# A hybrid decoder layer on one core: the instruction order taken from a simulation in time of queues and engines

## The chip, the cores and the metric

The kernel runs on one core of a Trainium2 chip. The metric is the device time of one execution in microseconds (us), the median of several runs. The engines are PE (TensorE, matmuls; PEld is its weight load), DVE (VectorE), ACT (ScalarE), POOL (GpSimd) and SP (SyncE, which here issues nearly all transfers). Each engine has its own list of instructions, and waits on semaphores for the others.

## The reference

One layer of a decoder with two groups of heads side by side, over 2048 tokens of width 1024, in float32:

```
h = rmsnorm(x);  z = h @ W_in                    # q, k, v and gates of both groups
FoX,   8 heads x 64:  softmax(q k^T * scale + c_t - c_s, causal) @ v
                      # c: running sum of log forget gates; swept in blocks of 128 queries
mLSTM, 4 heads x 128: 16 chunks of 128 tokens, each
       num = w_inter * (q @ C) + ((q k^T) * w_intra) @ v
       C   = decay * C + (wk * k)^T @ v          # carried from chunk to chunk
       h   = num / max(|den|, exp(-m))           # times sigmoid(output gate), after a norm
x += concat(groups) @ W_out
x += relu(rmsnorm(x) @ W_up)^2 @ W_down
x += sigmoid(rmsnorm(x) @ W_pg) * (p @ W_ple);   out = rmsnorm(x)
```

q and k of the mLSTM pass through a causal convolution of width 4 and a SiLU first.

## The kernel before

All of the layer is one function, hybrid_layer, written with a tile framework: the code names tiles from pools and issues operations in program order, and the framework's scheduler decides in which order each engine gets its instructions, and puts in the semaphore waits. A pool gives a tag a number of buffers (bufs); a new tile of that tag waits until the readers of the tile that had the buffer are done. Products with full precision are made from several f16 products (high and low parts, names with hl), three matmuls where there was one.

The stages, in the order of the program:

- Start: x is normalized in groups of four token blocks (squares yjk on ACT, yy on ACT and DVE, L181 to L201) and transposed on SP (yt); the weights of mLSTM head 0 are scaled (L140, L155), and the gates of all heads computed.
- mLSTM, heads 0 to 3. ml_z makes the projections of a head: zqk (matmuls at L260, 128x512, into u), zvo (L271, 128x256, into va by L454 on ACT and og by L455 on DVE), and the convolution of q and k on DVE (L469, L471, two tiles of 128x2048). All use the PSUM pool psz with 4 banks. qk has 4 buffers, so two heads; va and og have one for even and one for odd heads. Then the head's 16 chunks run (below).
- After the chunks of a head: a normalization on DVE (mrd, mss, mrr; L534 to L541), sixteen products (L544), mh on ACT and POOL (L546, L547), and on SP two transposes mT (L550) and two stores mixd (L552).
- FoX: fox_z makes v, k and q for two heads at a time (zv at L271, zfk and zfq at L260). fox_attn then takes each head's query blocks in pairs of 17 key blocks: s on PE (L798, L800), bias added and maximum on DVE (L806), exp on ACT (L821), f16 parts on ACT and POOL (ph, L826, L828), transposes pt on SP (L830, 17 for each head), and av on PE (L846). av trails s by LAG = 3 pairs. The projections of later heads, the per-layer embedding products (pp) and part of the output projection (om) are written between the pairs as fill.
- Output projection (L641), MLP (h at L1036, d at L1054), the gate (pg at L1007) and the final norm.

A chunk c of mLSTM head h, shortened:

```
A.activation(wt[:, c, :], wt[:, c, :], AF.Exp, ...)                        # L498
PE.matmul(sps, lhsT=k[:, cc], rhs=q[:, cc], ...)                           # L500 s
V.scalar_tensor_tensor(wt[:, c, :], sps, scale, wt[:, c, :], MULT, MULT)   # L501
PE.matmul(nps, lhsT=wt[:, c, :], rhs=va[:, c, :], ...)                     # L504 n
PE.matmul(ips, lhsT=q[:, cc], rhs=cst, ...)                                # L508 i
PE.transpose(out=kps, in_=k[:, cc], ...)                                   # L519 k
A.activation(kw, kps, AF.Copy, scale=w_k[:, c, h:h + 1])                   # L521
PE.matmul(cps, lhsT=kw, rhs=va[:, c, :], ...)                              # L523 c
V.scalar_tensor_tensor(cn, cst, dec[...], cps, MULT, ADD)                  # L526 cst
```

wt of a head is loaded by SP from mrow (L490) and has mneg added on DVE (L492) before the exp. wt and mh share one buffer: both are allocated with tag="w", bufs=1. What of the later projections stands on PE between these matmuls is the scheduler's choice; in the order before it spreads them over the chunks.

The scheduler is chosen where the tile framework is opened, in the function below.

## Time and profile before

| | us |
|---|---|
| time, median of 3 runs | 2955.1 (2953.64 to 2956.42) |
| the profiled execution: its own time | 2954.4 |
| its span | 2952.7 |
| PE busy | 2698.4 |
| DVE busy | 1621.7 |
| ACT busy | 1008.3 |
| POOL busy | 698.7 |

The profile is of one execution. Busy times are sums over the instructions of an engine; the span less the busy time of PE is the time in which PE waited or had nothing to do.

### The profile page before, as it was taken

Reading aid. Unit: us, or ns where it says so; the run is one execution under the profiler, and the core shown is the slowest. Engines: PE = TensorE matmul, PEld = TensorE weight load, DVE = VectorE, ACT = ScalarE, POOL = GpSimd, SP = SyncE. Lnnn points to the kernel's source line nnn. Section 1 sums busy time; section 2 is a strip of 40 time slices with the busy share of each in tenths; the row PEclk is TensorE's granted clock in tenths of the full one; section 3 lists DMA queues with packets and bytes.
Section 4 is the critical chain, followed back from the end, with each engine's and each line's share of the span. In section 5 each row is a group of like instructions: output and inputs, shape, how many; then the busy total and the mean of one; then the engine's idle time right before and its main releaser. Section 6 shows DMA issues by size and latency. Waiting matters only on the chain. (4 is left out here: it accounts for less than half of the span.)

```text
span 2952.7 us, 45034 instructions
## 1 busy us (share of the span) xinstructions
PE 2698.4 (91%) x18229; PEld 1507.1 (51%) x18229; DVE 1621.7 (55%) x3633; ACT 1008.3 (34%) x1686; POOL 698.7 (24%) x435
## 2 busy tenths in 40 slices
PE   4998999888878788788999999999999999999997
PEld 2756767555454554343344444444444444444686
DVE  6464654766757657556654444444444444445636
ACT  6244444465555555553411111111111111113532
POOL 1011110244343444343122111111212111111132
PEclk9999999989899989999999999999999999999999
DMA  9212220387686879996700000000000000002623
GB/s 243 45 44 59 58 47 20 94 167 137 139 166 133 165 169 219 196 205 222 148 29 29 29 29 16 28 15 29 29 29 29 29 29 16 28 15 43 143 69 136
DMA packets 535265, 256.36 MB, mean 87 GB/s; under 512 B 432784, under 2 KB 502672, under 8 KB 535056
## 3 DMA queue, kind: packets, MB, share of 16 engines
q1 hardware_dynamic: 525296, 236.66, 35.0%
q10 hardware_dynamic: 9760, 16.82, 1.8%
q8 instruction: 142, 2.33, 0.3%
q14 instruction: 67, 0.55, 0.1%
HBM read 113.88 MB, written 32.60 MB: 50 GB/s over the span
## 5 line engine op out<-in xcount | busy, mean ns | idle before, releaser
L1054 PE MATMUL d<-wd_hl,hid 128*128 128x512 f16 x3072 | 678.2, 380 | 8.4 <-DVE x L1059 8.2
L1036 PE MATMUL h<-y1t,wu_hl 128*128 128x512 f16 x3072 | 673.5, 379 | 0.5 <-issue 0.5
L1054 PEld LDWEIGHTS <-hid 128*128 128x128 f16 x3072 | 301.3, 98 | 375.0 <-issue 15.8
L1036 PEld LDWEIGHTS <-wu_hl 128*128 128x128 f16 x3072 | 300.5, 98 | 363.2 <-ACT y1y L200 1.0
L1059 DVE SCALAR_TENSOR_TENSOR x<-d,fac,x 128x512 f32<-128x512 f32 x512 | 373.8, 747 | 132.2 <-PE d L1054 131.8
L1044 POOL TENSOR_TENSOR hid<-r,hid 128x512 f16<-128x512 f32 x128 | 174.5, 1364 | 765.2 <-ACT hid L1043 659.1
L1042 DVE SCALAR_TENSOR_TENSOR r<-h,r 128x512 f32<-128x512 f32 x128 | 88.3, 690 | 458.2 <-ACT r L1040 458.1
L1040 ACT ACTIVATE r<-h 128x512 f32<-128x512 f32 x128 | 75.9, 594 | 766.8 <-PE h L1036 763.3
L828 POOL TENSOR_TENSOR ph<-sp,ph 128x1024 f16<-128x1024 f32 x119 | 255.9, 2164 | 283.3 <-ACT ph L826 219.3
L271 PEld LDWEIGHTS <-yt 128*128 128x128 f16 x3072 | 251.6, 101 | 40.1 <-issue 13.7
L260 PE MATMUL zqk<-yt,wqk_hl 128*128 128x512 f16 x768 | 188.7, 393 | 27.9 <-DMA yt<-yy 27.9
L821 ACT ACTIVATE sp<-sp,nb,fs 128x1024 f32<-128x1024 f32 (+3 forms) x192 | 177.9, 982 | 85.2 <-DVE nb L818 60.5
L798 PE MATMUL s<-K,Q 128*128 128x512 f16 (+3 forms) x320 | 117.9, 369 | 79.4 <-DVE mx L806 76.4
L846 PE MATMUL av<-vt,pt 128*128 128x65 f16 x1088 | 121.9, 199 | 67.3 <-DMA pt<-ph 55.6
L271 PE MATMUL zvo<-wvo_hl,yt 128*128 128x256 f16 x1536 | 175.0, 275 | 4.1 <-ACT wvo_hl L155 2.8
L1007 PE MATMUL pg<-wpg_hl,y2t 128*128 128x256 f16 x1536 | 171.0, 275 | 4.7 <-DVE x L1059 4.0
L1007 PEld LDWEIGHTS <-y2t 128*128 128x128 f16 x1536 | 151.6, 99 | 24.1 <-issue 5.1
L826 ACT CAST ph<-sp 128x1024 f16<-128x1024 f32 x136 | 137.8, 1038 | 67.9 <-DMA pt<-ph 62.6
L846 PEld LDWEIGHTS <-pt 128*128 128x128 f16 x1088 | 105.3, 100 | 75.1 <-DMA pt<-ph 67.8
L806 DVE CUSTOM_DVE_ANT_0 sp<-s,bias,mx 128x512 f32<-128x512 f32 (+2 forms) x192 | 124.5, 648 | 29.4 <-POOL ph L828 14.2
L260 PEld LDWEIGHTS <-wqk_hl 128*128 128x128 f16 x768 | 77.4, 101 | 105.5 <-ACT wqk_hl L155 25.9
L641 PEld LDWEIGHTS <-mix 128*128 128x128 f16 x768 | 76.4, 102 | 101.6 <-issue 27.7
(380 smaller groups left out, 3648.2 us busy)
## 6 DMA issues: line engine op xcount, KB each, us to landing
x<-in_x_dram SPq DMA_DIRECT2D x32, 512.0 KB, 5.8
wu_st<-in_w_up_dram SPq DMA_DIRECT2D x16, 1024.0 KB
wd_st<-in_w_down_dram SPq DMA_DIRECT2D x16, 1024.0 KB, 4.9
bias<-crow SPq DMA_DIRECT2D x16, 512.0 KB, 5.9
pled<-fox_st ACTq DMA_DIRECT2D x32, 256.0 KB, 2.8
wod<-spare ACTq DMA_DIRECT2D x32, 256.0 KB, 5.0
wos<-wod SPq DMA_DIRECT2D x32, 256.0 KB, 3.9
emb<-pled SPq DMA_DIRECT2D x32, 256.0 KB, 3.0
```

The source lines that it names most:

```text
L260: PE.matmul(ps, lhsT=hl[:, a, kt, m * P:(m + 1) * P], rhs=yT[g][b][:, kt, :], start=i == 0, stop=i == 3 * KT - 1)
L271: PE.matmul(ps[:, 0:n], lhsT=yT[g][b][:, kt, o:o + P], rhs=hl[:, a, kt, 0:n], start=i == 0, stop=i == 3 * KT - 1)
L806: V.tensor_tensor_reduce(out=st[u][:, o * P:(o + n) * P], in0=ps[:, 0:n * P], in1=bias[kb // 8][:, kb % 8 * P:(kb % 8 + n) * P], scale=1.0 ...
L821: A.activation(sl_, sl_, AF.Exp, bias=nb, scale=fs[:, 0:1])
L826: A.copy(ph[:, 0:1024], st[u])
L828: eng.tensor_sub(ph[:, 1024:2048], st[u], ph[:, 0:1024])
L846: PE.matmul(ar, lhsT=pt[:, o, :], rhs=vs[:, 0:65], start=kb == 0, stop=False)
L1007: PE.matmul(ps, lhsT=aT[t // 4][ya][:, kt, o:o + P], rhs=hl[:, wa, kt, :], start=i == 0, stop=i == 3 * KT - 1)
L1036: PE.matmul(ps, lhsT=wu[:, a, kt, m * P:(m + 1) * P], rhs=y1T[g][b][:, kt, :], start=i == 0, stop=i == 3 * KT - 1)
L1044: T.tensor_sub(hid[:, 1, m], r2, hid[:, 0, m])
L1054: PE.matmul(ps, lhsT=hid[:, a, m, t * P:(t + 1) * P], rhs=wd[:, b, m, hf * 512:(hf + 1) * 512], start=i == 0, stop=i == 5)
L1059: V.scalar_tensor_tensor(xs, ps, fac, xs, ALU.mult, ALU.add)
```

## The change

The scheduler is told to take its order from a simulation in time, in which queues and engines have durations, in place of its simple estimate. Nothing that is computed is changed: every instruction of before is there, on the same engine, and only the order on each engine and queue moves, with the waits that follow from it.

```diff
-    with tile.TileContext(nc) as tc:
+    with tile.TileContext(nc, schedule_with_timeline_sim=True) as tc:
         hybrid_layer(tc, *args)
```

First PE, chunk 9 of mLSTM head 1 (s1_9 is s of head 1, chunk 9; the trailing number only tells tiles apart; zqk2 is the projection of head 2), before:

```order
L500 MATMUL s1_9_2800<-qk1_0_2173,qk1_1_2179 128x128
L260 LDWEIGHTS wqk2_hl_2997
L260 MATMUL zqk2_1_1_3111<-yt1_210,wqk2_hl_2997 128x512
L260 LDWEIGHTS wqk2_hl_2997
L260 MATMUL zqk2_1_1_3111<-yt1_210,wqk2_hl_2997 128x512
L260 LDWEIGHTS wqk2_hl_2997
L260 MATMUL zqk2_1_1_3111<-yt1_210,wqk2_hl_2997 128x512
L504 MATMUL n1_9_2803<-va1_408,wt1_2617 128x129
L508 MATMUL i1_9_2805<-cst1_8_2797,qk1_0_2173 128x129
L519 MATMUL k1_9_2811<-ident_75,qk1_1_2179 128x128
```

The same place after the change:

```order
L500 MATMUL s1_9_2800<-qk1_0_2173,qk1_1_2179 128x128
L504 MATMUL n1_9_2803<-va1_408,wt1_2617 128x129
L508 MATMUL i1_9_2805<-cst1_8_2797,qk1_0_2173 128x129
L519 MATMUL k1_9_2811<-ident_75,qk1_1_2179 128x128
L523 MATMUL c1_9_2815<-va1_408,kw1_9_2813 128x129
L500 MATMUL s1_10_2820<-qk1_0_2173,qk1_1_2179 128x128
L504 MATMUL n1_10_2823<-va1_408,wt1_2617 128x129
```

Before, three pairs of weight load and matmul of zqk2 stand between s and n, and three more between k and c; after, the chunk's own matmuls stand directly behind each other, and zqk2 stands in earlier chunks.

DVE at the end of head 0 (wt0 of s0_15 is its last chunk; mrd0 and mss0 are the normalization; qk2 is the convolution of head 2), before:

```order
L501 SCALAR_TENSOR_TENSOR wt0_1551<-s0_15_1854,wt0_1551 128x128
L438 MEMSET va2_3026 128x16
L455 TENSOR_SCALAR og1_409<-zvo1_6_2347,invvo1_1958 128x128
L511 TENSOR_TENSOR num0_1554<-num0_1554,n0_15_1857 128x129
L534 SCALAR_TENSOR_TENSOR mrd0_1866<-num0_1554 128x16
L535 TENSOR_TENSOR mrd0_1866<-mrd0_1866,em_402 128x16
L536 RECIPROCAL mrd0_1866<-mrd0_1866 128x16
L537 TENSOR_TENSOR mss0_1555<-mss0_1555,mrd0_1866 128x16
```

The same place after the change:

```order
L501 SCALAR_TENSOR_TENSOR wt0_1551<-s0_15_1854,wt0_1551 128x128
L469 TENSOR_SCALAR qk2_0_3241<-u2_0_3029,gt_115 128x2048
L438 MEMSET va2_3026 128x16
L469 TENSOR_SCALAR qk2_1_3247<-u2_1_3031,gt_115 128x2048
L471 SCALAR_TENSOR_TENSOR qk2_0_3241<-u2_0_3029,gt_115,qk2_0_3241 128x2048
L511 TENSOR_TENSOR num0_1554<-num0_1554,n0_15_1857 128x129
L471 SCALAR_TENSOR_TENSOR qk2_1_3247<-u2_1_3031,gt_115,qk2_1_3247 128x2048
L471 SCALAR_TENSOR_TENSOR qk2_0_3241<-u2_0_3029,gt_115,qk2_0_3241 128x2048
L534 SCALAR_TENSOR_TENSOR mrd0_1866<-num0_1554 128x16
L471 SCALAR_TENSOR_TENSOR qk2_1_3247<-u2_1_3031,gt_115,qk2_1_3247 128x2048
L471 SCALAR_TENSOR_TENSOR qk2_0_3241<-u2_0_3029,gt_115,qk2_0_3241 128x2048
L535 TENSOR_TENSOR mrd0_1866<-mrd0_1866,em_402 128x16
```

The convolution of head 2 has moved between the last chunk of head 0 and the normalization of head 0; before, it stood behind L544. At the end of head 1 the convolution of head 3 stands in the same way.

PE at the end of mLSTM (i3_15 is its last matmul, zv0 the projection of v for the first FoX heads), before:

```order
L508 MATMUL i3_15_5061<-cst3_14_5053,qk3_0_4309 128x129
L271 LDWEIGHTS yt0_135
L271 MATMUL zv0_1_5333<-fox_hl_5118,yt0_135 128x128
L271 LDWEIGHTS yt0_135
L271 MATMUL zv0_1_5333<-fox_hl_5118,yt0_135 128x128
```

The same place after the change, where s0_15 is the first query block of FoX head 0:

```order
L508 MATMUL i3_15_5061<-cst3_14_5053,qk3_0_4309 128x129
L798 LDWEIGHTS Q0_5162
L798 MATMUL s0_15_0_0_5954<-K_5163,Q0_5162 128x512
L800 LDWEIGHTS Q0_5162
L800 MATMUL s0_15_0_0_5954<-KL_5164,Q0_5162 128x512
L798 LDWEIGHTS Q0_5162
L798 MATMUL s0_15_0_4_5959<-K_5163,Q0_5162 128x512
```

All of zv0, zfk0 and zfq1 now stands within the mLSTM chunks. On SP the two loads of bias (L890) still stand behind the transposes and stores of the last mLSTM head, as before.

## Rows read from the trace of the kernel before

**Rows 1.** Windows: span, busy (x count) of PE, PEld, DVE, ACT, POOL; clock, DMA share, GB/s.

```profile
183.50:518.20 334.70, 321.04 (x2269) 230.32 (x2269) 183.08 (x444) 154.44 (x410) 34.08 (x17) 0.97 0.19 44
518.20:584.40 66.20, 60.45 (x534) 37.02 (x532) 45.51 (x153) 26.35 (x44) 11.39 (x9) 1.00 0.31 85
584.40:1322.30 737.90, 587.97 (x6233) 361.47 (x6233) 472.99 (x1472) 401.39 (x515) 303.05 (x155) 0.92 0.83 168
...
1460.00:2767.00 1307.00, 1303.00 (x6053) 592.19 (x6052) 633.17 (x968) 239.19 (x351) 241.17 (x173) 1.00 0.10 30
...
sum 2952.70, PE 2698.44 PEld 1507.12 DVE 1621.67 ACT 1008.27 POOL 698.75; mean PE 385.49 PEld 215.30 DVE 231.67 ACT 144.04 POOL 99.82
```

**Rows 2.** Timeline of one mLSTM chunk: start, duration, engine, operation, [idle before it, releaser].

```profile
295.98 0.27 PE L519 MATMUL k<-ident,qk 128*128 128x128 f32 x1
...
296.09 0.81 PE L260 MATMUL zqk<-yt,wqk_hl 128*128 128x512 f16 x3
...
296.86 0.30 PEld L523 LDWEIGHTS c<-va,kw 128*128 128x128 f32 x2 [0.45 <-ACT kw L521]
...
297.99 0.30 PEld L504 LDWEIGHTS n<-va,wt 128*128 128x128 f32 x2 [0.27 <-DVE wt L501]
...
298.54 0.27 PE L519 MATMUL k<-ident,qk 128*128 128x128 f32 x1
```

**Rows 3.** Timelines of DVE and SP after mLSTM head 1.

```profile
318.77 4.29 DVE L544 SCALAR_TENSOR_TENSOR num<-num,mrr_r,og 128x128 f32<-128x128 f32 x16
...
333.93 0.43 SPq L490 DMA_DIRECT2D wt<-mrow  x1
```

**Rows 4.** Timeline of PE from mLSTM head 0 to head 1.

```profile
231.75 0.39 PE L508 MATMUL i<-cst,qk 128*128 128x129 f32 x2
231.98 23.74 PE L271 MATMUL zvo<-wvo_hl,yt 128*128 128x256 f16 x216
...
268.92 0.80 PE L504 MATMUL n<-va,wt 128*128 128x129 f32 x2 [12.33 <-DVE wt L501]
...
272.95 0.39 PE L504 MATMUL n<-va,wt 128*128 128x129 f32 x2
```

**Rows 5.** The two lines of the convolution: duration in ns (min/median/max), first and last start.

```profile
L469 DVE TENSOR_SCALAR qk<-u,gt x8: 1278/1283/4507, 113.1 to 435.2; 128x2048 f32<-128x2048 f32 x8
...
L471 DVE SCALAR_TENSOR_TENSOR qk<-u,gt,qk x24: 2341/2344/2353, 114.4 to 443.7; 128x2048 f32<-128x2048 f32 x24
```

**Rows 6.** Timelines from mLSTM to FoX; groups of the page (busy us, mean ns).

```profile
539.29 20.88 PE L260 MATMUL zfk<-yt,fox_hl 128*128 128x512 f16 x96
...
546.20 0.76 DVE L893 TENSOR_SCALAR bias<-bias,fs 128x1024 f32<-128x1024 f32 x1 [0.86 <-DMA bias<-crow]
...
571.54 2.37 ACT L821 ACTIVATE sp<-sp,nb,fs 128x1024 f32<-128x1024 f32 x2 [3.20 <-DVE nb L818]
...
L828 POOL TENSOR_TENSOR ph<-sp,ph 128x1024 f16<-128x1024 f32 x119 | 255.9, 2164 | 283.3 <-ACT ph L826 219.3
...
L806 DVE CUSTOM_DVE_ANT_0 sp<-s,bias,mx 128x512 f32<-128x512 f32 (+2 forms) x192 | 124.5, 648 | 29.4 <-POOL ph L828 14.2
```

**Rows 7.** Windows around the wait of rows 4: the last three columns are clock, DMA, GB/s.

```profile
256.60:268.90 12.30, 0.00 (x0) 0.00 (x0) 2.88 (x4) 0.76 (x3) 0.00 (x0) 0.60 0.46 106
268.90:272.70 3.80, 3.78 (x12) 2.48 (x13) 1.16 (x4) 3.18 (x12) 0.00 (x0) 0.50 0.00 0
272.70:320.00 47.30, 47.30 (x270) 28.16 (x269) 21.83 (x77) 24.30 (x74) 3.97 (x2) 1.00 0.08 23
```

**Rows 8.** Timelines of ACT and DVE at the start.

```profile
24.73 0.62 ACT L181 ACTIVATE yjk<-x 128x512 f32<-128x512 f32 x1
...
26.53 2.28 DVE L140 TENSOR_REDUCE wvo_mx<-wvo_st 128x16 f32<-128x2048 f32 x1
```

**Rows 9.** Waits in FoX, 584 to 1322 us: total us, times, longest.

```profile
PE s L798 <- DVE mx L806: 76.4, 43, 4.9
...
PE av L846 <- DMA pt<-ph: 55.6, 35, 6.6
```

## The prediction

> **What bounds the kernel now.** The change moves instructions between places on each engine and alters none, so I first split the span into stages by a table of busy time over seven stretches [rows 1]. TensorE (PE) is busy 2698.4 us of the 2952.7 us span, and the 254.3 us in which it is idle are what an order can win or lose. They are not spread evenly: 13.7 us in the mLSTM stretch (183.5 to 518.2 us), 5.8 us in the fill of FoX (518.2 to 584.4), 149.9 us in FoX (584.4 to 1322.3), 4.0 us in the MLP (1460 to 2767). So the MLP, 44% of the time, has next to nothing to give, mLSTM and the fill behind it can only lose, and a gain must come from FoX. I then read the order of the instructions in both kernels, and priced each place from the timeline of before.
>
> **mLSTM, the chunks.** A chunk is a chain: PE s, DVE wt, PE n and k, ACT kw, PE c, PE s of the next chunk. The rows [rows 2] show the period: k starts at 295.98 and again at 298.54 us, 2.57 us apart. In it PE has two gaps, s to n and k to c; in each the order before puts three matmuls of a later head's projection. Back to back such a matmul takes 20.88 / 96 = 0.2175 us [rows 6], three 0.65 us. What the reader is to see is that the weight load of n still waits 0.27 us on DVE and that of c 0.45 us on ACT, although PE has just done this fill: the fill is hidden in full, and without it the chunk would still take 2.57 us. The changed order takes fill as early as its buffers allow: the first chunks of a head have 2.5 to 6.8 us in a gap, where it lengthens the chunk by all beyond 0.65 us, and the last chunks have none. Counted over the four heads, 29 gaps s to n and 25 gaps k to c become empty: 54 x 0.65 = 35 us of hidden work comes out into the open. **+35 us** (bounds: 0, if PE's work elsewhere had been waiting anyway, and 45, if the partly filled gaps count too).
>
> **mLSTM, between heads.** The weights wt of the next head share a buffer with wt and mh of this one, so n of the next head waits for a chain: last i, DVE normalization (sixteen 128x128 products, 4.29 us), mh on ACT and POOL, two transposes and two stores on SP, and behind them SP's load of wt [rows 3]. From head 0 to 1 it lasts from 231.75 + 0.39 us to 268.92 us, 36.8 us [rows 4]; PE covers 23.74 us of it with zvo, and waits 12.3 us. At the other two transitions the order before has 58 and 61 us of fill by the count of its matmuls, more than the chain, so nothing waits. The changed order leaves 17.6, 17.9 and 13.4 us, since most of the projections are already done. Besides, at 0 to 1 and 1 to 2 the convolution of head h+2 now stands on DVE ahead of the normalization. It is two multiplications of 1.283 us and six steps of 2.344 us [rows 5], 16.6 us together; it is released when the last chunk has read the old q and k, so it runs just then, and everything behind it in the chain is late by it. The chains become 53.4, 53.4 and 36.8 us; PE's idle time is 35.8 + 35.5 + 23.4 = 94.7 us in place of 12.3 us: **+82 us**. Bounds: if the convolution comes out hidden, 33.2 us less (49); if the fill waits for PSUM that is freed only behind the normalization and then adds to the chain, some 10 us at each more (112). I take the middle, since the order on an engine is fixed.
>
> **To the first transpose of FoX.** Before, the 66.2 us from the last i (518.2) to the first pt (584.4) were covered by zv and zfk, 20.88 us of the latter alone [rows 6]; PE was idle 5.8 us. In the changed order all of it is done inside mLSTM (54 us more fill there), and s of FoX stands right behind the last i. But the bias that the reduce of s needs is loaded by SP behind the transposes of the last mLSTM head: it was scaled on DVE at 546.20 + 0.76 us, and a second one follows, 30 us behind 518.2. That chain is not shortened. Four reduces (0.65 us each), an exp (2.37 / 2), a copy of about as much and a subtraction on POOL (2.2) and their latencies make some 8.5 us more [rows 6]. In these 38.5 us PE has about 8 us of s, pp and zv; idle 30.5 us in place of 5.8: **+25 us** (bounds: 15 to 35). Seen from the clock on the wall, the stretch shortens by 28 us and mLSTM grows by 171, which is the same sum.
>
> **The clock.** In the one long wait of mLSTM the granted clock fell: it was 0.60 on the mean from 256.6 to 268.9 us, 0.50 (1.2 GHz) from 268.9 to 272.7, and 1.00 (2.4 GHz) behind it [rows 7]. There the step from n to n was 268.92 to 272.95, 4.03 us, against 2.57 us: 1.46 us more [rows 4]. Bounds for 29 bare chunks: 0, if PE's short pauses leave the clock up, and 29 x 1.46 = 42 us. Between them I take **+20 us**: FoX, where PE is busy 80% in short pieces, has a mean of 0.92 and the MLP without pauses 1.00 [rows 1], and a bare chunk has more pauses than FoX.
>
> The Trainium skill (TensorE: Matmul & The Clock Gate, section "A second HAM failure mode: psum-queue depth-cycling") says that frequent short idle times between groups of matmuls are enough to make the clock swing, and so speaks against this change. By that rule all bare chunks would run at the low clock and the sum would be 22 us higher. The trace agrees only by the 0.92 in FoX; no bare chunks are in it.
>
> **Start.** Four squares of ACT for the second token group (0.62 us each and a read of the sum) and a DVE reduce of 2.28 us now stand ahead of the first yy, for whose transposes PE waits at the start [rows 8]: 4 x 0.8 and a part of the reduce, **+4 us** (bounds 0 and 6).
>
> **FoX.** PE's biggest waits are for the reduce (76.4 us, 43 times) and for pt [rows 9]; 17 pt in each of 8 heads go through SP's queue, and the DMA engines are busy 0.83 of 737.9 us, 612 us. The changed order mixes s and av more finely and has as much fill there in the same stretch; the PE work that stands between the s of a row pair and its av is 17.5 us on the mean against 20.3 before, with less in heads 3, 5 and 7. So some waits for the reduce shrink, and some for pt grow. Bounds: 738 - 612 = 126 us gained, if the DMA engines never pause; 35 waits for pt times 2.8 us, 98 us lost, if each grows by all the lost cover. I take **-15 us**, a tenth of PE's idle time there. Out-projection, MLP and the gate keep their order but for a few groups: 0 (at most 6 us either way); the MLP's PE has 4.0 us to give.
>
> **Sum.** Against the own time of the profiled execution, 2954.4 us (span 2952.7 + 1.7; the median of the three runs is 0.7 us above): 2954.4 + 4 + 35 + 82 + 25 + 20 - 15 = 3105.4 us, 5% slower. The median takes the same sum: 3106.
>
> **Rivals.** (a) The low clock all through the bare chunks: +42 in place of +20, 3128 us. For it: 4.03 us [rows 4]. Against it: the clock was back 3.8 us after the wait, with only 0.65 us of fill in each gap. (b) FoX comes out much better, since the new order is fed by a timing of queues: half of its bound, -63, gives 3058 us. For it: 149.9 us of idle; against it: DMA at 0.83. (c) The convolution is hidden and the transitions cost 49: 3073 us. Against it: it stands ahead in DVE's own queue. (d) FoX worse, by +40 (the lost cover at the heads that have less): 3161 us. (e) The other side, not slower: FoX would have to give back all 151 us that the other terms and my -15 leave, and 15 more, from 738 to about 572 us. The DMA engines alone are busy 612 us there, PE 588 us. It decides only if DMA work of FoX shrinks by 40 us and PE's idle time vanishes, and I see no reason for either. (f) The order scarcely differs in effect, because engines start work when it is ready: against it, PE stood still 12.33 us for n [rows 4] with k and zqk next behind it in its order, so an engine doesn't pass over an instruction that waits.
>
> **Chances.** Forecast (3080 to 3120) 0.41, (a) 0.17, (b) 0.13, (c) 0.13, (d) 0.11, (e) 0.02, (f) 0.03. The likeliest gives 3105. The range takes in (a) to (c) and most of (d): 3040 to 3158; what is left out is 2 in 10 (half of b and d, e, f). A measurement of this kernel can tell some 0.2% (6 us) from no change: faster 0.02, no change 0.03, slower 0.95.
>
> **What would show it.** In the changed trace: the first n at about 188 us; the last i of mLSTM at some 700 (505 us behind the first n, and up to 12 of the clock's 20), with PE waits of 36, 36 and 23 us on wt at the three transitions; two DVE convolution steps between the last wt and the normalization at the first two; the last six or so chunks of each head without zqk or zvo rows, at 2.57 us each (or 3.5 to 4 at clock 0.5, which is rival a); the first pt 38 us behind the last i; FoX between 690 and 760 us long; the MLP 1307 us as before. If transitions are short, the step on DVE's order failed; if FoX is below 680 us, the step on FoX; if the last chunks run faster than 2.57 us, the fill was not hidden, as I hold.

## The result and the profile after

The changed kernel takes 3154.1 us (median of four runs, 3147.7 to 3159.5) against 2954.6 us: a ratio of 1.068, 95% interval 1.0661 to 1.0698. It is 200 us slower, within the range by 4 us, and 49 us above the likeliest value. The windows of the changed kernel, cut at the same events as [rows 1], read like those rows (span; busy time and count of PE, PEld, DVE, ACT, POOL; clock; DMA share; GB/s). The stages are the start, mLSTM, the way to the first pt, FoX, the output projection, the MLP and the gate:

```profile
0.00:199.30 199.30, 144.06 (x1158) 88.27 (x1158) 95.07 (x214) 75.68 (x134) 23.38 (x22) 0.94 0.48 118
199.30:746.20 546.90, 412.91 (x2768) 297.58 (x2769) 213.47 (x532) 169.92 (x438) 44.02 (x27) 0.82 0.13 32
746.20:787.10 40.90, 13.04 (x62) 5.72 (x62) 26.43 (x85) 15.31 (x22) 8.06 (x3) 0.62 0.34 93
787.10:1519.30 732.20, 575.69 (x6183) 360.42 (x6181) 468.18 (x1441) 398.36 (x510) 297.30 (x151) 0.90 0.81 168
1519.30:1657.00 137.70, 128.16 (x574) 56.76 (x572) 97.28 (x199) 49.30 (x94) 39.77 (x26) 0.97 0.77 197
1657.00:2964.00 1307.00, 1292.41 (x5987) 586.33 (x5986) 631.90 (x970) 238.49 (x353) 239.00 (x172) 1.00 0.10 30
...
sum 3153.20, PE 2733.24 PEld 1543.33 DVE 1624.32 ACT 1006.73 POOL 701.72; mean PE 390.46 PEld 220.48 DVE 232.05 ACT 143.82 POOL 100.25
```

The span is 200.5 us longer. PE is busy 34.8 us more with the same instructions (2733.2 against 2698.4), which is the work that fell into stretches of low clock, and idle 165.7 us more (420.0 against 254.3). By stage, the idle time (span less PE) changed as follows: start 45.2 to 55.2; mLSTM 13.7 to 134.0; to the first pt 5.8 to 27.9; FoX 149.9 to 156.5; the rest 39.7 to 46.4. So 120 of the 166 us are in mLSTM, and its clock, 0.97 before, is 0.82.

What PE waited for in the mLSTM stretch, 199.3 to 746.2 us (us in total, times, longest):

```profile
PE zvo L271 <- DVE og L455: 49.1, 2, 26.1
PE n L504 <- DVE wt L501: 49.0, 34, 9.5
PE c L523 <- ACT kw L521: 23.8, 27, 5.9
PE zv L271 <- DVE Q L748: 13.1, 1, 13.1
```

The first and the last row are the transitions, where fill stands in PE's list but its PSUM is freed only behind the normalization. Of the second row 23.2 us are the ends of the three transitions (5.55, 8.13 and 9.53 us); the rest of it, and the third row, are waits inside the chunks, most of them chunks without fill. Before, n waited for wt twice in all that stretch. The rows of PE at the transition 0 to 1, which answer to [rows 4]:

```profile
317.64 0.64 PE L508 MATMUL i<-cst,qk 128*128 128x129 f32 x2
...
344.85 20.60 PE L271 MATMUL zvo<-wvo_hl,yt 128*128 128x256 f16 x161 [26.14 <-DVE og L455]
371.01 0.80 PE L504 MATMUL n<-va,wt 128*128 128x129 f32 x2 [5.55 <-DVE wt L501]
```

From the end of i to the next n it lasts 52.7 us (53.4 from its start), where the chain was priced at 53.4, and PE waits 31.7 us of it. The other two wait 31.1 and 22.6 us. DVE shows why:

```profile
316.91 1.28 DVE L469 TENSOR_SCALAR qk<-u,gt 128x2048 f32<-128x2048 f32 x1
...
334.36 2.34 DVE L471 SCALAR_TENSOR_TENSOR qk<-u,gt,qk 128x2048 f32<-128x2048 f32 x1
...
340.12 4.29 DVE L544 SCALAR_TENSOR_TENSOR num<-num,mrr_r,og 128x128 f32<-128x128 f32 x16
```

The convolution of head 2 runs from 316.91 us, and L544, the step of [rows 3], begins only at 340.12, 22.5 us behind the start of the last i. The last chunks of head 3 are bare (timeline of PE, answering to [rows 2]):

```profile
739.76 0.80 PE L523 MATMUL c<-va,kw 128*128 128x129 f32 x2 [0.52 <-ACT kw L521]
740.35 0.64 PE L500 MATMUL s<-qk,qk 128*128 128x128 f32 x2
741.37 0.80 PE L504 MATMUL n<-va,wt 128*128 128x129 f32 x2 [0.38 <-DVE wt L501]
741.97 0.64 PE L508 MATMUL i<-cst,qk 128*128 128x129 f32 x2
742.39 0.42 PE L519 MATMUL k<-ident,qk 128*128 128x128 f32 x1
743.33 0.80 PE L523 MATMUL c<-va,kw 128*128 128x129 f32 x2 [0.52 <-ACT kw L521]
...
775.83 0.59 PE L798 MATMUL s<-K,Q 128*128 128x512 f16 x1 [26.48 <-DVE mx L806]
```

c follows c after 3.57 us, where a chunk took 2.57 with fill in it; k lasts 0.42 us where it took 0.27 [rows 2]. The last row is FoX's wait for the bias behind mLSTM, with no fill left in front of it.

### The profile page after: what moved, and what is told of

Its sections match the earlier page's. It is cut to its first block, busy times and chain, and to the rows that moved or that the text cites. A ratio compares the mean times of both kernels' runs of the same rounds, so it can differ in the third digit from the quotient of the medians.

```text
span 3153.2 us, 45028 instructions
## 1 busy us (share of the span) xinstructions
PE 2733.2 (87%) x18229; PEld 1543.3 (49%) x18229; DVE 1624.3 (52%) x3633; ACT 1006.7 (32%) x1686; POOL 701.7 (22%) x435
## 5 line engine op out<-in xcount | busy, mean ns | idle before, releaser
L1054 PE MATMUL d<-wd_hl,hid 128*128 128x512 f16 x3072 | 689.3, 380 | 16.0 <-DVE x L1059 16.0
L1036 PE MATMUL h<-y1t,wu_hl 128*128 128x512 f16 x3072 | 686.2, 379 | 0.0
L271 PE MATMUL zvo<-wvo_hl,yt 128*128 128x256 f16 x1536 | 182.2, 280 | 49.5 <-DVE og L455 49.1
L260 PE MATMUL zqk<-yt,wqk_hl 128*128 128x512 f16 x768 | 176.8, 389 | 30.3 <-DMA yt<-yy 28.3
L846 PE MATMUL av<-vt,pt 128*128 128x65 f16 x1088 | 135.8, 205 | 67.9 <-DMA pt<-ph 56.0
L847 PE MATMUL av<-vt,pt 128*128 128x64 f16 x1088 | 135.8, 206 | 0.0
```

The lines of the kernel that those rows point to most:

```text
L260: PE.matmul(ps, lhsT=hl[:, a, kt, m * P:(m + 1) * P], rhs=yT[g][b][:, kt, :], start=i == 0, stop=i == 3 * KT - 1)
L271: PE.matmul(ps[:, 0:n], lhsT=yT[g][b][:, kt, o:o + P], rhs=hl[:, a, kt, 0:n], start=i == 0, stop=i == 3 * KT - 1)
L846: PE.matmul(ar, lhsT=pt[:, o, :], rhs=vs[:, 0:65], start=kb == 0, stop=False)
L847: PE.matmul(ar[:, 1:65], lhsT=pt[:, o, :], rhs=vs[:, 65:129], start=False, stop=False, skip_group_check=True)
L1036: PE.matmul(ps, lhsT=wu[:, a, kt, m * P:(m + 1) * P], rhs=y1T[g][b][:, kt, :], start=i == 0, stop=i == 3 * KT - 1)
L1054: PE.matmul(ps, lhsT=hid[:, a, m, t * P:(t + 1) * P], rhs=wd[:, b, m, hf * 512:(hf + 1) * 512], start=i == 0, stop=i == 5)
```

## The experiments

Each kernel is timed beside the kernel before, which took 2947.1 to 2949.2 us in these runs, 5 to 8 us less than beside the changed kernel; the changed kernel was not timed again. So each time below has its distance from the kernel before beside it, to be held against the 199.5 us of the changed kernel. Where no interval stands, the kernel was run once. The four runs of the changed kernel span 12 us, and FoX alone, with the same order on PE, took 728.0 to 740.7 us in four traces (changed kernel, e2_zvo, e4_warm, e12_gate) and 729.7 to 737.8 in three (before, e8_bare, e10_cover); a difference of such a size in the time shows nothing by itself, and the trace of mLSTM or of the start carries the verdict. "n to n" is worked out from the starts of n. "Held behind" is an edge of order on the same engine, without a wait.

**The convolution behind the normalization** (e1_conv). In the changed kernel:

```diff
+            with behind(last_n.get(h - 2)):      # last L544 of head h-2, on DVE
                 V.tensor_scalar(o, u[:, 0:S], wc[:, 0, ci:ci + 1], None, op0=ALU.mult)
                 for j in range(1, 4):
                     V.scalar_tensor_tensor(o, u[:, j:j + S], wc[:, j, ci:ci + 1], o, ...)
```

> The order from the simulation, but the convolution of head h+2 is held behind the normalization of head h on DVE (order only). If the convolution's place lengthens the chain between heads by its 16.6 us at 0 to 1 and at 1 to 2, the last i to the next n falls there from 53.9 and 52.1 us to about 37, and the time from 3154 to about 3121 us. If that chain is set by the fill on PE (the last zvo of the transition waiting for its buffers) or by the DMA of wt, the two transitions stay above 50 us and the time stays within 6 us of 3154.

Measured 3133.6 us, 184.9 above the kernel before. n to n fell from 54.0 to 38.2 us at 0 to 1 and from 52.1 to 37.1 at 1 to 2 (39.1 and 38.8 at 2 to 3, which the edit doesn't touch). PE at 0 to 1:

```profile
330.67 20.10 PE L271 MATMUL zvo<-wvo_hl,yt 128*128 128x256 f16 x162 [14.35 <-DVE og L459]
...
352.90 0.49 PE L509 MATMUL n<-va,wt 128*128 128x129 f32 x2 [2.14 <-DVE wt L506]
```

The waits are 14.35 and 2.14 us in place of 26.14 and 5.55. mLSTM (first n to last i) shortened by 35 us, as expected. FoX and the stretch from it to the first h took 10 and 9 us more, in orders that the scheduler changed too, so the time above the kernel before fell by 15 us.

**zvo in the transitions** (e2_zvo). In the changed kernel:

```diff
         if h > 0:
-            for g in range(G):
-                zvo(g)
+            with behind(last_i[h - 1]):           # last i of head h-1, on PE
+                for g in range(G):
+                    zvo(g)
```

> The order from the simulation, but all of zvo of head h is held on PE behind the last i of head h-1, so 41.9 us of fill stand in each transition. If a transition costs what its chain (37 us) lasts beyond the fill that stands in it, PE's waits at the three transitions (31.7, 31 and 22.6 us) go, the fill leaves the chunks where it was exposed, more chunks become bare (39 in place of 28), and the sum of the prediction with 1.0 us for each bare chunk at the low clock gives mLSTM 460 us in place of 529 (547 measured): about 3085 us. If run-ahead of fill costs nothing and the time is lost otherwise, 3154.

Measured 3136.4 us, 187.8 above the kernel before: 12 us better than the changed kernel, not 69; mLSTM is 19 us shorter. The waits at the transitions did go, as expected; they now last 51.3, 55.2 and 54.4 us, but of work that begins at the low clock. What was missing was a second cost: with no fill in head 0, its first chunks took 8.7, 8.6 and 7.4 us, not 3.57. PE and DVE there:

```profile
208.35 0.80 PE L509 MATMUL n<-va,wt 128*128 128x129 f32 x2 [3.15 <-DVE wt L506]
...
216.92 0.80 PE L509 MATMUL n<-va,wt 128*128 128x129 f32 x2 [5.34 <-DVE wt L506]
```

```profile
208.01 0.28 DVE L506 SCALAR_TENSOR_TENSOR wt<-s,wt 128x128 f32<-128x128 f32 x1
208.21 1.28 DVE L473 TENSOR_SCALAR qk<-u,gt 128x2048 f32<-128x2048 f32 x1
209.40 2.28 DVE L156 TENSOR_TENSOR wqk_hl<-wqk_st,wqk_hl 128x2048 f16<-128x2048 f32 x1
211.60 2.34 DVE L475 SCALAR_TENSOR_TENSOR qk<-u,gt,qk 128x2048 f32<-128x2048 f32 x1
```

Long DVE steps of other heads stand between two wt of the chunks, and without fill PE has nothing to do meanwhile. My estimate had priced a bare chunk by its own chain alone.

**Extra matmuls, written into s and k** (e4_warm). In the changed kernel, for chunks 9 to 15; the computed values are unchanged, the added results unused:

```diff
                 PE.matmul(sps[:, 0:P], lhsT=k[:, cc], rhs=q[:, cc], start=True, stop=True)
+                if c >= 9:     # 4 x 128x384 f16 into sps[:, P:512]; the same behind k into kps
+                    warm(sps)
```

> The order from the simulation, with four extra f16 matmuls of 128x384 (about 0.64 us, their results unused) behind s and behind k in the chunks 9 to 15 of each head. If a bare chunk lasts 3.57 us only since PE runs at the low clock there, it falls to about 2.6 us though PE does more, some 25 us over the 27 bare chunks less 6 where fill stands as well: about 3131 us. If 3.57 us are the chunk's own chain, the extra work is hidden at best: 3154 to 3170 us, and bare chunks of 3.57 us or more.

Measured 3180.1 us, 231.5 above the kernel before, and as a test it failed: since the added matmuls write the tile of s, wt on DVE waited for them, and they joined the chain. It still compares the two clocks on one chain: such chunks took 6.13 us at a granted clock of 0.50 and 3.73 us at the high one. Three of the first kind and one of the second in head 1 (clock is the third column from the end):

```profile
458.50:476.89 18.39, 15.68 (x51) 9.11 (x52) 5.15 (x21) 3.07 (x12) 2.27 (x2) 0.50 0.10 29
481.12:484.85 3.73, 2.83 (x17) 1.77 (x17) 0.93 (x3) 1.02 (x4) 0.00 (x0) 1.00 0.02 4
```

In each of them PE pauses 0.90 us in two pieces, as long as in a bare chunk at the low clock, and yet the clock came back. So the length of the pauses alone doesn't decide.

**Extra matmuls beside the chain** (e7_warm). The same in chunks 10 to 15, with five of 128x256 into free columns of the tiles of n and c, held behind s and k:

```diff
+                if c >= 10:
+                    warm(nps, ms)       # behind s; likewise warm(cps, mk) behind k
                 PE.matmul(nps[:, 0:MD + 1], lhsT=wt[:, c, :], rhs=va[:, c, :], ...)
```

> The order from the simulation, with five extra f16 matmuls of 128x256 (0.55 us, results unused) behind s and behind k in the chunks 10 to 15 of each head, written where no other engine waits for them (into free columns of the tiles of n and of c), so that they lie in the gaps of the chunk. If a bare chunk lasts 3.57 us since PE runs at its low clock there, and keeping PE busy in the gaps keeps the clock up, the late chunks fall to about 2.6 us at a granted clock of 1.0, some 20 us in all; heads with real fill in chunk 10 and later pay up to 1.1 us for each such chunk. If keeping PE busy that much doesn't bring the clock back, they stay at 3.57 us or more at a clock of 0.5.

Measured 3145.6 us, 198.5 above the kernel before. The late chunks of head 1 (start of s to start of s) went from 3.57 us each to 3.64, 3.01 and then 2.2 us; heads 2 and 3 also end at 2.2 us. Two windows in head 1, the first while the clock rises, the second behind it (clock is the third column from the end):

```profile
455.00:462.00 7.00, 7.00 (x42) 5.95 (x41) 3.61 (x15) 2.34 (x10) 0.38 (x1) 0.64 0.26 75
462.00:467.00 5.00, 5.00 (x46) 4.60 (x44) 2.58 (x13) 2.06 (x8) 0.00 (x0) 1.00 0.01 3
```

With PE kept busy the clock comes back to 1.00, and chunks with more work in them are faster. That they go below 2.57 us is another effect: here the scheduler put s of the next chunk ahead of c. mLSTM shortened by 20 us, as expected; FoX and the stretch from it to the first h took 8.0 and 5.5 us more, in an order of FoX that the scheduler changed too, and the time above the kernel before is the same.

**Bare chunks in the order of before** (e8_bare). In the kernel before, with zqk and zvo of head 3 held behind the last i of head 2:

```diff
-            for g in range(G):
-                zqk(g)
+            with behind(last_i.get(h - 1) if h == 3 else None):
+                for g in range(G):
+                    zqk(g)                        # and likewise zvo
```

> The order of before, with the fill of mLSTM head 2 (zqk and zvo of head 3) held behind the last i of head 2, so its 16 chunks are bare and 22 us more of fill stand in the transition 2 to 3, which has more fill than its chain anyway. By the prediction 31 gaps x 0.65 = 20 us of work come out into the open, and the low clock adds 1.0 us for each bare chunk, up to 15 us: 20 to 35 us slower, 2970 to 2985. If the fill of before was not hidden and the chunk is shorter without it, less than 10 us.

Measured 2984.1 us, ratio 1.0134 (1.0117 to 1.0151): 37 us above the kernel before, where 20 to 35 were expected. All chunks of head 2 but the first went from mostly 2.56 to 3.57 us, so that its n to n sum is 54.3 in place of 40.5 us, and the transition behind it lasts 87.9 in place of 62.5. The window of the 16 bare chunks:

```profile
372.00:424.00 52.00, 38.47 (x131) 28.43 (x131) 17.11 (x53) 17.64 (x58) 2.27 (x2) 0.50 0.04 11
```

PE is busy 38.5 of 52 us there and the granted clock stays at 0.50 all through. One edit in the order of before so shows both terms in its trace, the exposed fill (25 us with its slow beginning) and the clock (14 us).

**The split of one weight** (e9_prep). In the changed kernel, one ACT and one DVE instruction:

```diff
+        late = name == "wfv0"                     # a FoX weight; A.copy(mh) and L544 of head 1
+        with behind(last_a[1] if late else None), behind(last_n[1] if late else None):
             A.copy(hl[:, 0], sf)
             V.tensor_sub(hl[:, 1], sf, hl[:, 0])
```

> The order from the simulation, with one thing moved: the split of a FoX weight (wfv0) into f16 parts, one ACT and one DVE instruction, is held behind the normalization of head 1; in the changed order DVE's part stands ahead of wt in a late chunk of head 1, and wt and n waited 8 us for it. If that wait is the split's place, the chunk of 11.2 us falls to some 4 us, and the time by about 8 us to 3146. If wt waited for something else there, the chunk stays at 11 us.

In the changed kernel POOL, ACT, DVE and PE stood there as follows:

```profile
451.18 1.89 POOL L149 TENSOR_TENSOR fox_st<-fox_st,wfv_gs 128x1024 f32<-128x1024 f32 x1 [7.14 <-issue]
453.10 1.04 ACT L155 CAST fox_hl<-fox_st 128x1024 f16<-128x1024 f32 x1 [6.86 <-POOL fox_st L149]
454.17 1.23 DVE L156 TENSOR_TENSOR fox_hl<-fox_st,fox_hl 128x1024 f16<-128x1024 f32 x1 [6.42 <-ACT fox_hl L155]
455.32 0.28 DVE L501 SCALAR_TENSOR_TENSOR wt<-s,wt 128x128 f32<-128x128 f32 x1
455.66 0.80 PE L504 MATMUL n<-va,wt 128*128 128x129 f32 x2 [8.07 <-DVE wt L501]
```

The wait begins on POOL: its product that scales the weight starts 7.14 us behind the reduction in front of it, ACT's part of the split waits for the product, DVE's part for ACT's, and wt stands behind that in DVE's list.

With the edit the wait is gone, and the chunks behind it are these (PE):

```profile
444.60 0.49 PE L511 MATMUL n<-va,wt 128*128 128x129 f32 x2 [0.42 <-DVE wt L508]
447.17 0.49 PE L511 MATMUL n<-va,wt 128*128 128x129 f32 x2 [0.42 <-DVE wt L508]
449.73 0.50 PE L511 MATMUL n<-va,wt 128*128 128x129 f32 x2 [0.42 <-DVE wt L508]
```

The chunk of 11.20 us fell to 3.55 us, and head 1 from 106.1 to 96.4 us. Without the long wait the clock was even up for two bare chunks: 2.57 and 2.56 us apart, the same instructions that take 3.57 at the low clock. The local cause, the place of the split, is shown (POOL's product still starts 6.85 us behind its reduction there). The gain in time was not: 3170.6 us, ratio 1.0761 (1.0743 to 1.0779), 223.5 above the kernel before and so 24 us worse than the changed kernel; FoX took 10 us and the stretch behind it 10 us more. The edit moved the scheduler's order of FoX as well; beyond that I have no cause for those 20 us.

**The fill of mLSTM put back by hand** (e6_spread). The changed kernel with the edits of e1_conv and, on PE, a ration of fill for each gap:

```diff
+    NQ, NV, NF = 3, 5, 9          # matmuls of zqk, zvo, zv held behind each s and each k
+            with spread(h - 1, NQ) if h > 1 else nullcontext():      # zqk of head h
+            with spread(0, NV) if h == 1 else behind(last_i[h - 1]): # zvo of head h
+            with spread(MH - 1, NF) if j == 0 else nullcontext():    # zv0; zfk0 behind last i
```

> The order from the simulation, with the fill of mLSTM held by hand to about the places it had before: 5 zvo matmuls of head 1 in each gap of head 0, 3 zqk matmuls in each gap of heads 1 and 2, 9 zv in each of head 3, the rest of it in the transitions, and the convolution behind the normalization; all else in the order from the simulation. If the loss is where the prediction puts it, mLSTM falls from 547 to about 341 us (335 before) and the time to 2950 to 2965 us, with only the start (some 9 us of idle time) against the kernel before. If a good part of the loss is elsewhere, it stays above 2990.

Measured 3031.9 us, ratio 1.0288 (1.0269 to 1.0306), 83 us above the kernel before: 116 of the 200 us are regained by where mLSTM's fill and convolution stand, but not all of it, as was expected. mLSTM fell from 547 to 386 us, not to 341. In the first chunks of head 0 n waits for wt behind the convolution of head 1 on DVE (3.79 and 2.94 us; three chunks of 9.9, 7.4 and 7.6 us), the transition 2 to 3 took 75.2 us, and head 3 got fill of zfq ahead of its ration. FoX took 14 us more than before, the start 17. Of what is left, mLSTM with the way to the first pt still holds 34 us (435 against 401 before), so "a good part of the loss elsewhere" holds for some 50 us at most.

**zv0 and zfk0 behind mLSTM** (e11_fox). In the changed kernel:

```diff
+            with behind(last_i[MH - 1] if j == 0 else None):         # last i of mLSTM, on PE
                 ps = z_token(hv, t, f"zv{j}_{t}", P)                  # zv; likewise zfk
```

> The order from the simulation, with zv0 and zfk0 (42 us of fill) held on PE behind the last i of mLSTM, where PE waited some 28 us for the bias of FoX; zfq1 moves behind them by itself, so head 3 of mLSTM runs bare. If the wait for the bias is a cost of having no fill left there, head 3 falls from 96 to some 54 us (15 bare chunks at 3.57 us), the way from the last i to the first av grows from 46 to some 62 us without a wait in it, and FoX takes 0 to 21 us of zfq1: 7 to 28 us faster, 3126 to 3147. If fill costs the same wherever it stands, no change.

Measured 3179.5 us, 230.4 above the kernel before: 31 us worse. Head 3 fell from 96.1 to 56.1 us, all but its first chunk at 3.57 us; from the last i to the first av it took 73.6 us in place of 46.4, with PE busy nearly throughout. mLSTM and the way to the first pt are together 16 us shorter. The wait for the bias is covered, and the gain was lost again in FoX, which took 34 us more from first to last av; 32 of them are in its head 0 (98.4 us in place of 66.4), where PE was busy 16 us more and idle 16 us more. Only 13 of the 96 matmuls of zfq1 stand in FoX, so they can't be the cause; the scheduler gave FoX another order, with more of pp and zv in head 0, and which of its waits makes the loss is open.

**POOL's order at the start** (e12_gate). In the changed kernel:

```diff
+        with behind(red[0] if name == "wqk2" else None):      # the gates' reduction (L385)
             pw, sc = pow2_scale(mp, npart, name)
             ...
             T.tensor_mul(st, st, gs.unsqueeze(3).to_broadcast([P, kn, npart, wd]))
```

> The order from the simulation, with POOL's two steps of the weight wqk2 (a reduction over partitions and a product) held behind POOL's reduction for the gates, as they stood before; all other engines keep their order. In the changed kernel the gates' reduction starts at 175.1 us behind them, against 160.1 before. If that order on POOL is what delays the first n (199.3 against 183.5 us), the reduction starts near 162 us, the wait of 8.8 us on PE at 167 us goes, and the first n comes 7 to 12 us earlier: 3142 to 3147. If the first n is late for the transposes at the start (4.3 us) and the fill ahead of it (7 us), it moves by less than 3 us.

Measured 3141.8 us, 192.6 above the kernel before: 7 us better than the changed kernel. The trace carries the verdict: the first n is at 185.8 us in place of 199.3, and PE's idle time ahead of it, 55.2 us in the changed kernel and 45.2 before, is 45.0. POOL in the changed kernel, and then with the edit:

```profile
157.88 0.37 POOL L114 PARTITION_ALL_REDUCE wqk_al<-wqk_mp  x1 [12.47 <-DVE wqk_mp L144]
165.58 3.60 POOL L149 TENSOR_TENSOR wqk_st<-wqk_st,wqk_gs 128x2048 f32<-128x2048 f32 x1 [7.33 <-issue]
175.13 0.54 POOL L385 PARTITION_ALL_REDUCE scr<-a_s  x1 [5.96 <-issue]
```

```profile
159.88 0.55 POOL L393 PARTITION_ALL_REDUCE scr<-a_s  x1 [13.95 <-DVE a_s L390]
160.35 0.47 POOL L114 PARTITION_ALL_REDUCE wqk_al<-wqk_mp  x1
167.65 3.60 POOL L156 TENSOR_TENSOR wqk_st<-wqk_st,wqk_gs 128x2048 f32<-128x2048 f32 x1 [6.83 <-issue]
```

Two instructions on POOL ahead of the gates' reduction held up the first chunk; of the squares and the DVE reduce that I had priced, no idle time is left to be seen.

**More cover in the order of before** (e10_cover), the one attempt at a version that beats both:

```diff
+            if h == 2:       # n of head 1, chunk 0, behind the 58th matmul of zqk of head 2
+                tc.add_manual_dep(first_n[1], pe[57].name, ...)
```

> The order of before, with the first n of head 1 held on PE behind 57 matmuls of zqk of head 2, so that 12.4 us more of fill stand in the transition 0 to 1, where PE waited 12.3 us; what is moved there is missing in the transition 1 to 2 (7 us), which had more fill than its chain, and in early chunks of head 1, where it was in the open. If a transition costs what its chain lasts beyond its fill, the time falls by 10 to 14 us, to 2936 to 2940 on the chip of the runs before. If the work is hidden where it was, no change.

Measured 2957.9 us, ratio 1.0043 (1.0029 to 1.0058): 11 us slower, not 10 to 14 faster. The wait of 12.3 us at 0 to 1 is gone, and two others came in its place:

```profile
277.00 0.80 PE L530 MATMUL c<-va,kw 128*128 128x129 f32 x2 [7.94 <-ACT kw L528]
...
344.18 5.05 PE L271 MATMUL zvo<-wvo_hl,yt 128*128 128x256 f16 x23 [7.48 <-DVE og L455]
```

kw stands on ACT behind the sigmoid of og and a cast of wvo that the scheduler moved ahead of it, and og on DVE behind four steps of the convolution. No version here beats the kernel before.

## Why the prediction was right, and where its size was off

- **Transitions** (+82): 85.4 us of waits in place of 12.3, so +73. Chains of 52.7, 50.8 and 37.8 us (end of the last i to the next n) were priced at 53.4, 53.4 and 36.8; e1_conv shows the convolution's part. The rival that it comes out hidden is refuted.
- **Bare chunks and clock** (+35 and +20): here the sum was 27 us short. Outside the transitions mLSTM's idle time grew from 1.4 to 48.6 us, and PE's busy time by 34.8 us: 82 us in place of 55. The bare chunks themselves came out near their price. By the trace 25 chunks (n to n) have no fill: two take 2.56 us at the high clock, 16 take 3.57 us at the low one, and seven more take 4.0 to 8.3 us, at the low clock for all or part of it. So the low clock nearly all through, the condition of rival (a), is what happened, but at 1.0 us for each of 23 chunks, some 23 us at most and not 42: the 1.46 us read from [rows 4] is the price of a chunk with fill in its gaps. The fill that came out is 25 x 1.3 = 33 us.

  What the sum had at nothing is a chunk's waits for long steps of other work in the queues that it crosses. Of the 48.6 us of idle time about 23 are the chunks' own pauses (0.90 us in each at the low clock) and some 26 are longer waits: 8.1 in head 1 (shown by e9_prep), 2.8 and 5.9 in head 3 (read from the trace, not tried), the rest in pieces of up to 1.5 us. Together that is an estimate of 82 us (33, 23 and 26). The last wait of head 3:

```profile
717.51 1.89 POOL L149 TENSOR_TENSOR fox_st<-fox_st,wfk_gs 128x1024 f32<-128x1024 f32 x1 [6.71 <-issue]
719.42 1.04 ACT L155 CAST fox_hl<-fox_st 128x1024 f16<-128x1024 f32 x1 [6.78 <-POOL fox_st L149]
721.05 0.80 PE L523 MATMUL c<-va,kw 128*128 128x129 f32 x2 [5.88 <-ACT kw L521]
```

  All three begin, as in e9_prep's rows, with a weight's product on POOL that starts some 7 us behind a reduction, while ACT's split waits for it; behind the split stand kw on ACT, or DVE's part of it with wt. The Trainium skill (TensorE: Matmul & The Clock Gate, section "A second HAM failure mode: psum-queue depth-cycling") has short pauses make the clock swing; these chunks bear it out in that the clock fell with no pause above 0.61 us in the chunks ahead (e9_prep), but it then stayed at 0.50 and did not swing.
- **To the first pt** (+25): +22, and 40.9 us for the stretch against 38.5. Right in size, though e11_fox shows that covering it doesn't win it back.
- **Start** (+4): +10, all of which went with POOL's order (e12_gate); I had read DVE's and ACT's order there and not POOL's.
- **FoX** (-15): the step that failed. The order does mix more finely, and nothing was gained: 732.2 against 737.9 us is within what the same orders vary by, and PE was busy 12 us less, so idle 7 us more. The waits that were to shrink did not:

```profile
PE s L798 <- DVE mx L806: 73.9, 37, 6.1
...
PE av L846 <- DMA pt<-ph: 56.0, 36, 3.8
```

  They were 76.4 and 55.6 us [rows 9]. By the starts of pt, head 0 became 18 us and head 7 11 us shorter, as fill left them (zfq1 had been done in mLSTM, om in earlier heads), and heads 1 to 4 some 26 us longer. The windows by head show where: head 2 has 11 us more PE work in it, and heads 3 and 5, where less fill stands, have PE idle for 23.0 and 31.7 us in place of 13.5 and 17.0 (in the same order, 23.6 and 31.9 in e12_gate; before, 13.1 and 15.8 in e8_bare), while head 6 has 10 us less. So the lost cover that rival (d) named is there, and other heads pay most of it back.
- **The rest** (0): +7, of which 8.4 us are one wait of the MLP's d for x at 1664 us.

Summed, the errors are start 6, mLSTM 18, FoX 22, the rest 7, less 3 for the first pt: 50 us, the whole of the difference. Rivals b, c and d (much better FoX, hidden convolution, much worse FoX) are out, and so is f; e was never near. That 3154 lies within the range is in part luck: its upper end, 3158, allowed for a loss in FoX that didn't come, and what filled it was waits in mLSTM that no rival named.

## What to carry to other kernels

Fill that a scheduler may take early should be rationed where it covers a latency chain: work that hides 0.65 us in each of a hundred gaps is worth its whole length there and nothing where PE would be busy anyway, so count the fill in each gap and each long wait of the order, and sum the idle time by stage. Read every queue that the chain crosses, POOL's and ACT's too, for long steps of other work between two short ones of the chain, and for steps that wait for another engine. A cover that is moved must be paid from somewhere that was exposed, and three of the four attempts here to add cover by hand met a new wait behind it.

## What the runs showed of the hardware

A bare chunk keeps PE busy 38.5 of 52 us in e8_bare, with pauses of about 0.4 and 0.5 us, and the granted clock stayed at 0.50 (1.2 GHz) for all 52 us, while FoX, with PE busy 79% in the mean, had 0.90. Directly behind dense work one or two such chunks ran at 2.56 us at the high clock, and then the clock fell (changed kernel, e9_prep). With the same pauses and four more matmuls behind s and behind k it came back, after three chunks of e4_warm at 0.50. On POOL a product that followed a reduction over partitions began some 7 us later with no other wait shown (7.33, 7.14, 6.83 and 6.71 us), and a reduction behind a product 6 us later (5.96).
